# Row-wise argmax: the last tiles in column pieces with a VectorE lookup, and 128 chunks of 64 elements per row in place of 64 of 128

## The chip, the cores and the metric

The kernel runs on one core of a Trainium2 chip. The metric is the device time of one execution in microseconds (us); each kernel was executed several times, and this text quotes medians. The profile of one execution gives the span, from the first to the last instruction, which here is about 1.8 us shorter than the device time.

Names: VectorE is DVE in the profile, GpSimd is POOL, ScalarE is ACT, TensorE is PE, SyncE's queue is SPq. "xt" is a tile of input: 128 rows of 8192 float32, 4 MB. There are 64 such tiles, 0 to 63.

## The reference

```python
def setup_inputs():
    return {"x": np.random.randn(8192, 8192).astype(np.float32)}

def reference(x):
    return np.argmax(x, axis=1)
```

The output is int64, so the kernel writes each index as a pair of int32 words, the upper one zero.

## The kernel before

A row is cut into C chunks of L = 8192 / C elements. VectorE reduces each tile to C chunk maxima per row (`cm`), in one instruction for the whole tile, and that is nearly all its work. Per group of four tiles, a lookup follows: the row maximum `mx`, the first chunk that holds it (GpSimd compares and multiplies with a descending ramp, VectorE takes the maximum `k`), an indirect DMA that fetches that one chunk per row from HBM again (`ga`), and the same match inside the chunk. Each step is put some tiles later in program order, so that VectorE does not wait for GpSimd or for the gather.

```python
C = 64;  L = M // C                      # 64 chunks of 128
groups = [4] * 15 + [2, 1, 1]
# (constants, buffers, keep(), some arguments, store() and the group's last step are cut)

def stage2(t0, g, cm, now):
    reduce_max(out=mx, in_=cm)                       # VectorE
    w, k = first_match(cm, mx, descC, C, g, "c")     # GpSimd, two operations per tile
    def stage3():                                    # one tile later
        reduce_max(out=k, in_=w)                     # VectorE
        tensor_tensor(out=idx, in0=base[:, t0:t0 + g], in1=k, op=ALU.subtract)
        for i in range(g):
            nc.gpsimd.indirect_dma_start(out=ga[:, i, :], in_=x_flat, ... idx[:, i:i + 1] ...)
        w2, k2 = first_match(ga, mx, descL, L, g, "l")
        # (stage4, four tiles later: reduce w2 to k2, combine with k into res; cut)

for g in groups:
    for i in range(g):
        parts = 4 if t == NT - 1 else 1              # only tile 63 is loaded in pieces
        # (one DMA per part into xt, then one reduce_max per part into cm)
        run_due(t)
        t += 1
    stage2(t0, g, cm, t - 1)
# (the rest of the steps, then transpose, cast and store of the last four tiles)
```

Five buffers hold tiles, so loads run up to five tiles ahead.

## Time and profile before

| | before |
|---|---|
| time, median of the first three runs (with a fourth, used below, 667.21) | 667.33 us (667.04 to 667.47) |
| span of the profiled run | 665.3 us |
| last x packet ends (the trace's DMA packets) | 639.8 us |
| last reduce of x ends | 648.1 us |
| from there to the end of the span | 17.2 us |

The first lines are from the page of the kernel before: the span, the busy tenths of VectorE and of the DMA engines in 40 slices of the span, and the two DMA queues with packets, megabytes and share of the 16 engines' time. Queue q1 carries x, q0 the gathers (half of q0's 2048 packets are of 4 bytes; the other 1024 carry the rows).

```profile
span 665.3 us, 723 instructions
...
DVE  2899898998989899898998989899898998989891
...
DMA  9999999999999999999999999999999999999930
...
q1 hardware_dynamic: 9731, 268.51, 94.5%
q0 software_dynamic: 2048, 4.20, 1.7%
```

The DMA engines are at 9 tenths for 38 slices and then nearly idle for the last two. VectorE is nearly as full, 8 or 9 tenths from the second slice to the last but one.

The groups by shape (line, engine, operation, output and input, count; busy us and mean ns of one; idle time just before them and what ended it):

```profile
L135 DVE TENSOR_REDUCE cm<-xt 128x64 f32<-128x8192 f32 x63 | 547.0, 8683 | 65.9 <-DMA xt<-in_x_dram 65.9
...
L135 DVE TENSOR_REDUCE cm<-xt 128x16 f32<-128x2048 f32 x4 | 8.9, 2274 | 0.0
```

A whole tile takes VectorE 8.68 us. A quarter takes 2.27 us; four in a row took 8.85 (in the timeline below), 0.17 more than a whole tile, because the records of successive reduces overlap a little. Taken at 0.96 GHz, 8192 elements are 8.53 us and 2048 are 2.13, which leaves 0.15 and 0.14 us per instruction. The Trainium skill ("VectorE: DVE Perf Modes", Specifications and the section on the TRN2 errata) gives that clock and a measured fixed term of about 150 cycles, 0.156 us; this trace agrees with both, to within 0.02 us.

The timeline of the tail (start, duration, engine, line, operation, count; in brackets the idle time before and what ended it):

```profile
630.11 8.69 DVE L135 TENSOR_REDUCE cm<-xt 128x64 f32<-128x8192 f32 x1 [2.05 <-DMA xt<-in_x_dram]
...
639.23 8.85 DVE L135 TENSOR_REDUCE cm<-xt 128x16 f32<-128x2048 f32 x4
...
649.93 1.05 POOL L102 DMA_INDIRECT ga<-in_x_dram,idx  x1 [4.57 <-DVE mx L93]
...
655.27 1.04 POOL L102 DMA_INDIRECT ga<-in_x_dram,idx  x1 [0.73 <-DVE idx L99]
...
658.00 0.62 POOL L63 TENSOR_SCALAR w<-ga,mx 128x128 f32<-128x128 f32 x1 [1.69 <-DMA ga<-in_x_dram,idx]
...
659.19 0.29 DVE L108 TENSOR_REDUCE k<-w 128x1 f32<-128x128 f32 x1 [2.90 <-POOL w L65]
...
660.38 0.26 ACT L88 CAST o<-ps 4x128 int32<-4x128 f32 x1 [10.47 <-PE ps L85]
```

Tile 62 is reduced from 630.11 on, the four pieces of tile 63 only behind it, until 648.08. Then the two last groups of one tile take their gathers in turn (649.93 and 655.27), each with a GpSimd match, and after the last come match, reduce, transpose, cast (660.38) and store.

### The profile page before, as it was taken

The page shows a single profiled execution, that of the slowest core. Times are in us where ns is not written, and L with a number is a line of the kernel's source. Part 1 is how long each engine was busy: PE and PEld are TensorE (multiplying, and loading weights), DVE is VectorE, ACT ScalarE, POOL GpSimd, SP SyncE. Part 2 cuts the span into 40 slices and gives each one's busy share as a digit, 9 for nine tenths or more (in the row PEclk, how much of TensorE's full clock was granted, in tenths as well). Part 3 has the DMA queues.
Part 4 walks back from the last instruction along what each step waited for, and adds up shares of the span by engine and source line. Part 5 has one row for each costly group of instructions (what it writes and reads, how often), then busy time and mean ns, then how long its engine had stood idle before and what let it go on. Part 6 is the DMA issues. An engine that isn't in the chain of part 4 may idle for free.

```text
span 665.3 us, 723 instructions
## 1 busy us (share of the span) xinstructions
PE 0.8 (0%) x2; PEld 0.2 (0%) x2; DVE 584.1 (88%) x175; ACT 1.8 (0%) x3; POOL 179.7 (27%) x331
## 2 busy tenths in 40 slices
PE   0000000000000000000000000000000000000000
PEld 0000000000000000000000000000000000000000
DVE  2899898998989899898998989899898998989891
ACT  0000000000000000000000000000000000000000
POOL 1004214041231304214032231304214131331442
DMA  9999999999999999999999999999999999999930
GB/s 378 441 428 425 424 441 426 426 431 420 439 426 428 426 426 440 423 430 420 430 423 442 431 418 430 425 440 418 430 431 426 439 421 430 428 426 439 405 161 12
DMA packets 11786, 272.75 MB, mean 410 GB/s; under 512 B 2116, under 2 KB 2180, under 8 KB 3204
## 3 DMA queue, kind: packets, MB, share of 16 engines
q1 hardware_dynamic: 9731, 268.51, 94.5%
q0 software_dynamic: 2048, 4.20, 1.7%
q14 instruction: 7, 0.05, 0.0%
HBM read 272.63 MB, written 0.07 MB: 410 GB/s over the span
## 4 chain that ended last, share of the span: by engine, by line
DMA 76%; DVE 19%; issue 3%; POOL 0%; SPq 0%; POOLq 0%; PE 0%; ACT 0%; DVEq 0%; ACTq 0%
DMA xt<-in_x_dram 75%; DVE cm L135 18%; DMA ga<-in_x_dram,idx 1%; DVE k L108 0%; SPq L132 0%; POOL w L63 0%; DVE mx L93 0%; DVE k L97 0%; DVE res L110 0%; POOL w L65 0%; DVE res L112 0%; POOLq L171 0%; DVE idx L99 0%; PE ps L85 0%; ACT o L88 0%
## 5 line engine op out<-in xcount | busy, mean ns | idle before, releaser
L135 DVE TENSOR_REDUCE cm<-xt 128x64 f32<-128x8192 f32 (+1 forms) x67 | 555.9, 8301 | 65.9 <-DMA xt<-in_x_dram 65.9
L63 POOL TENSOR_SCALAR w<-cm,mx 128x64 f32<-128x64 f32 x64 | 28.2, 441 | 261.4 <-DVE mx L93 261.4
L102 POOL DMA_INDIRECT ga<-in_x_dram,idx x64 | 62.4, 974 | 115.0 <-DVE idx L99 91.2
L63 POOL TENSOR_SCALAR w<-ga,mx 128x128 f32<-128x128 f32 x64 | 38.8, 606 | 91.7 <-DMA ga<-in_x_dram,idx 91.7
L65 POOL TENSOR_TENSOR w<-w,descL 128x128 f32<-128x128 f32 x64 | 29.1, 454 | 5.3
L65 POOL TENSOR_TENSOR w<-w,descC 128x64 f32<-128x64 f32 x64 | 20.4, 319 | 5.3
L108 DVE TENSOR_REDUCE k<-w 128x4 f32<-128x512 f32 (+2 forms) x18 | 11.1, 617 | 2.9 <-POOL w L65 2.9
L97 DVE TENSOR_REDUCE k<-w 128x4 f32<-128x256 f32 (+2 forms) x18 | 6.8, 379 | 4.8 <-POOL w L65 4.8
L93 DVE TENSOR_REDUCE mx<-cm 128x4 f32<-128x256 f32 (+2 forms) x18 | 6.9, 382 | 0.1
L99 DVE TENSOR_TENSOR idx<-base,k 128x4 uint32<-128x4 f32 (+2 forms) x18 | 2.9, 162 | 0.9 <-DVE k L97 0.3
L112 DVE TENSOR_SCALAR res<-res 128x4 f32<-128x4 f32 (+2 forms) x18 | 3.0, 168 | 0.6
L110 DVE SCALAR_TENSOR_TENSOR res<-k 128x4 f32<-128x4 f32 (+2 forms) x18 | 2.9, 162 | 0.6
L88 ACT CAST o<-ps 60x128 int32<-60x128 f32 (+1 forms) x2 | 0.5, 263 | 658.1 <-PE ps L85 658.1
L85 PE MATMUL ps<-ident,res 128*60 128x128 f32 (+1 forms) x2 | 0.8, 382 | 659.5 <-DVE k L97 649.2
L88 ACT ACT_TABLE_LOAD x1 | 1.3, 1283 | 0.7 <-PEq L160 0.7
L87 POOL MEMSET o<- 60x256 int32 (+1 forms) x2 | 0.6, 301 | 0.0
L55 POOL TENSOR_SCALAR ident<-ident 128x128 f32<-128x128 f32 x1 | 0.5, 534 | 0.0
L85 PEld LDWEIGHTS ps<-ident,res 128*60 128x60 f32 (+1 forms) x2 | 0.2, 104 | 659.8 <-issue 649.2
L42 POOL IOTA descC<- 128x64 f32 x1 | 0.2, 175 | 0.4 <-POOLq L160 0.4
L45 POOL IOTA descL<- 128x128 f32 x1 | 0.2, 228 | 0.0
L53 POOL IOTA ident<- 128x128 f32 x1 | 0.2, 228 | 0.0
L49 POOL IOTA base<- 128x64 f32 x1 | 0.2, 174 | 0.0
(4 smaller groups left out, 0.4 us busy)
## 6 DMA issues: line engine op xcount, KB each, us to landing
xt<-in_x_dram SPq DMA_DIRECT2D x63, 4096.0 KB, 41.0
xt<-in_x_dram SPq DMA_DIRECT2D x4, 1024.0 KB, 37.5
ga<-in_x_dram,idx POOLq DMA_INDIRECT x64, 8.6
out_dram<-o SPq DMA_DIRECT2D x1, 60.0 KB, 1.6
out_dram<-o SPq DMA_DIRECT2D x1, 4.0 KB
```

What stands on the lines that cost most here:

```text
L63: keep(nc.gpsimd.tensor_scalar(out=w[:, i, :], in0=vals[:, i, :], scalar1=mx[:, i:i + 1], scalar2=None, op0=ALU.is_equal))
L65: keep(nc.gpsimd.tensor_tensor(out=w[:, i, :], in0=w[:, i, :], in1=desc, op=ALU.mult))
L85: nc.tensor.transpose(ps, res[:, t0:t0 + n], ident)
L88: nc.scalar.copy(out=o[:, :, 0:1], in_=ps.unsqueeze(2))
L93: keep(nc.vector.reduce_max(out=mx, in_=cm, axis=AX.X))
L97: keep(nc.vector.reduce_max(out=k, in_=w, axis=AX.X))
L99: keep(nc.vector.tensor_tensor(out=idx, in0=base[:, t0:t0 + g], in1=k, op=ALU.subtract))
L102: keep(nc.gpsimd.indirect_dma_start(out=ga[:, i, :], out_offset=None, in_=x_flat[:, :], in_offset=bass.IndirectOffsetOnAxis(ap=idx[:, i:i ...
L108: keep(nc.vector.reduce_max(out=k2, in_=w2, axis=AX.X))
L110: keep(nc.vector.scalar_tensor_tensor(out=res[:, t0:t0 + g], in0=k, scalar=float(L), in1=k2, op0=ALU.mult, op1=ALU.add))
L112: keep(nc.vector.tensor_scalar(out=res[:, t0:t0 + g], in0=res[:, t0:t0 + g], scalar1=-1.0, scalar2=float(C * L + L), op0=ALU.mult, op1=ALU ...
L135: keep(nc.vector.reduce_max(out=cm[:, i, q * cw:(q + 1) * cw], in_=xt[:, q * w:(q + 1) * w].rearrange("p (c l) -> p c l", c=cw), axis=AX.X))
```

## The change

Its intent: (A) 128 chunks of 64, so that the gathers fetch half the bytes; (B) the last four tiles loaded and reduced in column pieces of 2048 and less, so that VectorE can start on a tile before all of it has landed; (C) tiles 62 and 63 looked up by VectorE alone (`max` and `max_index`), without GpSimd's matches, and tile 63 stored directly without a transpose. The core of the diff:

```diff
-    C = 64
+    C = 128
@@ load and reduce, in pieces @@
+    def load_reduce(t, cm, widths):
+        for w in widths:
+            keep(nc.sync.dma_start(out=xt[:, at:at + w], in_=x[t * P:(t + 1) * P, at:at + w]))
+        for w in widths:
+            keep(nc.vector.reduce_max(out=cm[:, c0:c1], in_=xt[:, at:at + w]..., axis=AX.X))
+            step[0] = t * 4 + at // 2048      # deferred steps now count quarter tiles
+            run_due()
@@ lookup of one tile on VectorE @@
+    def direct_begin(t, cm):
+        keep(nc.vector.max(out=m8, in_=cm))
+        keep(nc.vector.max_index(out=c8, in_max=m8, in_values=cm))
+        keep(nc.vector.tensor_tensor(out=idx, in0=c8[:, 0:1], in1=base[:, t:t + 1], op=ALU.add))
+        keep(nc.gpsimd.indirect_dma_start(out=ga, ..., in_=x_flat[:, :], ... idx ...))
+    def direct_end(m8, c8, ga, dst):
+        keep(nc.vector.max_index(out=l8, in_max=m8, in_values=ga))
+        keep(nc.vector.scalar_tensor_tensor(out=dst, in0=c8[:, 0:1], scalar=float(L), in1=l8[:, 0:1], ...))
@@ order @@
-    groups = [4] * 15 + [2, 1, 1]
+    for g in [4] * 15 + [2]:
+            load_reduce(t, cm[:, i, :], [M] if t < 60 else [2048] * 4)
+        lookup(t0, g, cm, 4, 7) if g == 4 else lookup(t0, g, cm, 1, 100)
+    load_reduce(62, cm62, [2048] * 4);                     d62 = direct_begin(62, cm62)
+    load_reduce(63, cm63, [2048] * 3 + [1024, 512, 512]);  d63 = direct_begin(63, cm63)
+    step[0] = 1000;  run_due()
+    direct_end(*d62, res[:, 62:63]);  store(60, 3)
+    direct_end(*d63, o_last[:, 0:1]); nc.sync.dma_start(out=out_pairs[63 * P:, :], in_=o_last)
```

More of the change, by code (lines that the diff above doesn't have):

```diff
@@ L35, with out_view @@
     oth = out.tensor
-    oth2 = type(oth)(name=oth.name, shape=[NT, 2 * P], dtype=I32, base_partition=oth.base_partition)
-    out_i32 = oth2.ap()
+    def out_view(shape):
+        return type(oth)(name=oth.name, shape=shape, dtype=I32, base_partition=oth.base_partition).ap()
+    out_rows = out_view([NT, 2 * P])
+    out_pairs = out_view([N, 2])
     x_flat = x.tensor.reshape([N * C, L]).ap()
@@ L48 @@
     base = cpool.tile([P, NT], F32)
-    nc.gpsimd.iota(out=base, pattern=[[P * C, NT]], base=C, channel_multiplier=C,
+    nc.gpsimd.iota(out=base, pattern=[[P * C, NT]], base=0, channel_multiplier=C,
+                   allow_small_or_imprecise_dtypes=True)
+    baseC = cpool.tile([P, NT], F32)
+    nc.gpsimd.iota(out=baseC, pattern=[[P * C, NT]], base=C, channel_multiplier=C,
                    allow_small_or_imprecise_dtypes=True)
@@ L57, with defer, run_due, match @@
     res = cpool.tile([P, NT], F32)
-    def first_match(vals, mx, desc, n, g, name):
-        w = spool.tile([P, g, n], F32, tag=f"w_{name}")
+    o_last = cpool.tile([P, 2], I32)
+    nc.gpsimd.memset(o_last, 0)
+    pending = []
+    step = [0]
+    def defer(steps, fn):
+        pending.append((step[0] + steps, fn))
+        pending.sort(key=lambda e: e[0])
+    def run_due():
+        while pending and pending[0][0] <= step[0]:
+            pending.pop(0)[1]()
+    def load_reduce(t, cm, widths):
+        assert sum(widths) == M
+        xt = xpool.tile([P, M], F32, tag="xt")
+        at = 0
+        for w in widths:
+            keep(nc.sync.dma_start(out=xt[:, at:at + w], in_=x[t * P:(t + 1) * P, at:at + w]))
+            at += w
+        at = 0
+        for w in widths:
+            c0, c1 = at // L, (at + w) // L
+            keep(nc.vector.reduce_max(
+                out=cm[:, c0:c1], in_=xt[:, at:at + w].rearrange("p (c l) -> p c l", l=L), axis=AX.X))
+            at += w
+            step[0] = t * 4 + at // 2048
+            run_due()
+    def match(w, vals, mx, desc, g):
         for i in range(g):
             keep(nc.gpsimd.tensor_scalar(out=w[:, i, :], in0=vals[:, i, :], scalar1=mx[:, i:i + 1],
-                                    scalar2=None, op0=ALU.is_equal))
+                                         scalar2=None, op0=ALU.is_equal))
             keep(nc.gpsimd.tensor_tensor(out=w[:, i, :], in0=w[:, i, :], in1=desc, op=ALU.mult))
-        k = spool.tile([P, g], F32, tag=f"k_{name}")
-        return w, k
-    groups = [4] * 15 + [2, 1, 1]
-    assert sum(groups) == NT
-    pending = []
-    def run_due(now, all_=False):
-        while pending and (all_ or pending[0][0] <= now):
-            pending.pop(0)[1]()
-    def defer(due, fn):
-        pending.append((due, fn))
-        pending.sort(key=lambda e: e[0])
     def store(t0, n):
@@ L85, in store, with lookup, gather @@
         nc.tensor.transpose(ps, res[:, t0:t0 + n], ident)
-        o = spool.tile([n, P, 2], I32, tag="o")
+        o = cpool.tile([n, P, 2], I32, tag=f"o{t0}")
         nc.gpsimd.memset(o, 0)
-        nc.scalar.copy(out=o[:, :, 0:1], in_=ps.unsqueeze(2))
-        keep(nc.sync.dma_start(out=out_i32[t0:t0 + n, :], in_=o.rearrange("t p two -> t (p two)")))
-    def stage2(t0, g, cm, now):
+        keep(nc.scalar.copy(out=o[:, :, 0:1], in_=ps.unsqueeze(2)))
+        keep(nc.scalar.dma_start(out=out_rows[t0:t0 + n, :], in_=o.rearrange("t p two -> t (p two)")))
+    def lookup(t0, g, cm, gather_after, match_after):
         mx = spool.tile([P, g], F32, tag="mx")
         keep(nc.vector.reduce_max(out=mx, in_=cm, axis=AX.X))
-        w, k = first_match(cm, mx, descC, C, g, "c")
-        def stage3():
-            keep(nc.vector.reduce_max(out=k, in_=w, axis=AX.X))
+        wc = spool.tile([P, g, C], F32, tag="wc")
+        match(wc, cm, mx, descC, g)
+        k = spool.tile([P, g], F32, tag="k")
+        def gather():
+            keep(nc.vector.reduce_max(out=k, in_=wc, axis=AX.X))
             idx = spool.tile([P, g], U32, tag="idx")
-            keep(nc.vector.tensor_tensor(out=idx, in0=base[:, t0:t0 + g], in1=k, op=ALU.subtract))
+            keep(nc.vector.tensor_tensor(out=idx, in0=baseC[:, t0:t0 + g], in1=k, op=ALU.subtract))
             ga = spool.tile([P, g, L], F32, tag="ga")
@@ L104, in stage3 @@
                     in_offset=bass.IndirectOffsetOnAxis(ap=idx[:, i:i + 1], axis=0)))
-            w2, k2 = first_match(ga, mx, descL, L, g, "l")
-            def stage4():
-                keep(nc.vector.reduce_max(out=k2, in_=w2, axis=AX.X))
-                keep(nc.vector.scalar_tensor_tensor(out=res[:, t0:t0 + g], in0=k, scalar=float(L),
-                                               in1=k2, op0=ALU.mult, op1=ALU.add))
-                keep(nc.vector.tensor_scalar(out=res[:, t0:t0 + g], in0=res[:, t0:t0 + g],
-                                        scalar1=-1.0, scalar2=float(C * L + L),
-                                        op0=ALU.mult, op1=ALU.add))
+            wl = spool.tile([P, g, L], F32, tag="wl")
@@ new lines, in gather, with finish @@
+            match(wl, ga, mx, descL, g)
+            def finish():
+                k2 = spool.tile([P, g], F32, tag="k2")
+                keep(nc.vector.reduce_max(out=k2, in_=wl, axis=AX.X))
+                r = res[:, t0:t0 + g]
+                keep(nc.vector.scalar_tensor_tensor(out=r, in0=k, scalar=float(L), in1=k2,
+                                                    op0=ALU.mult, op1=ALU.add))
+                keep(nc.vector.tensor_scalar(out=r, in0=r, scalar1=-1.0, scalar2=float(C * L + L),
+                                             op0=ALU.mult, op1=ALU.add))
@@ L115, in stage4 @@
                 if t0 + g == 60:
                     store(0, 60)
-            defer(now + 4, stage4)
-        defer(now + 1, stage3)
+            defer(match_after, finish)
+        defer(gather_after, gather)
+    def direct_begin(t, cm):
+        m8 = spool.tile([P, 8], F32, tag="m8")
+        keep(nc.vector.max(out=m8, in_=cm))
+        c8 = spool.tile([P, 8], U32, tag="c8")
+        keep(nc.vector.max_index(out=c8, in_max=m8, in_values=cm))
+        idx = spool.tile([P, 1], U32, tag="idx1")
+        keep(nc.vector.tensor_tensor(out=idx, in0=c8[:, 0:1], in1=base[:, t:t + 1], op=ALU.add))
+        ga = spool.tile([P, L], F32, tag="ga1")
+        keep(nc.gpsimd.indirect_dma_start(
+            out=ga, out_offset=None, in_=x_flat[:, :],
+            in_offset=bass.IndirectOffsetOnAxis(ap=idx[:, :1], axis=0)))
+        return m8, c8, ga
@@ L122 @@
+    def direct_end(m8, c8, ga, dst):
+        l8 = spool.tile([P, 8], U32, tag="l8")
+        keep(nc.vector.max_index(out=l8, in_max=m8, in_values=ga))
+        keep(nc.vector.scalar_tensor_tensor(out=dst, in0=c8[:, 0:1], scalar=float(L), in1=l8[:, 0:1],
+                                            op0=ALU.mult, op1=ALU.add))
     t = 0
-    for g in groups:
+    for g in [4] * 15 + [2]:
         cm = spool.tile([P, g, C], F32, tag="cm")
@@ L126 @@
         for i in range(g):
-            xt = xpool.tile([P, M], F32, tag="xt")
-            parts = 4 if t == NT - 1 else 1
-            w = M // parts
-            cw = C // parts
-            for q in range(parts):
-                keep(nc.sync.dma_start(out=xt[:, q * w:(q + 1) * w],
-                                  in_=x[t * P:(t + 1) * P, q * w:(q + 1) * w]))
-            for q in range(parts):
-                keep(nc.vector.reduce_max(
-                    out=cm[:, i, q * cw:(q + 1) * cw],
-                    in_=xt[:, q * w:(q + 1) * w].rearrange("p (c l) -> p c l", c=cw), axis=AX.X))
-            run_due(t)
-            t += 1
-        now = t - 1
-        stage2(t0, g, cm, now)
-    run_due(0, all_=True)
-    while pending:
-        run_due(0, all_=True)
-    store(60, NT - 60)
+            load_reduce(t, cm[:, i, :], [M] if t < 60 else [2048] * 4)
+            t += 1
+        if g == 4:
+            lookup(t0, g, cm, 4, 7)
+        else:
+            lookup(t0, g, cm, 1, 100)
+    cm62 = spool.tile([P, C], F32, tag="cm1")
+    load_reduce(62, cm62, [2048] * 4)
+    d62 = direct_begin(62, cm62)
+    cm63 = spool.tile([P, C], F32, tag="cm1")
+    load_reduce(63, cm63, [2048] * 3 + [1024, 512, 512])
+    d63 = direct_begin(63, cm63)
+    step[0] = 1000
+    run_due()
+    direct_end(*d62, res[:, 62:63])
+    store(60, 3)
+    direct_end(*d63, o_last[:, 0:1])
+    nc.sync.dma_start(out=out_pairs[63 * P:, :], in_=o_last)
 _INS = ['x']
```

## The prediction

> **What bounds it now.** Two stages. Until about 640 us the DMA engines are the limit: the table of 40 slices shows DMA at 9 tenths through slice 38, and the windows from 12 to 594 us show a DMA share of 1.00 to 1.01 at 426 to 431 GB/s, with VectorE busy 91%. In the groups by shape VectorE needs 8.68 us for a 4 MB row tile; a tile lands every 9.7 us; the idle time before it (65.9 us) all ends on xt. Then comes a serial tail of 26 us: in the trace's DMA packets the last x packet ends at 639.8 us, the span at 665.3. In the timeline that tail is VectorE reducing the last tile (639.2 to 648.1, as its four pieces queue behind tile 62, reduced whole until 638.8), two gather rounds in turn (649.9 and 655.3), POOL matches, a transpose, a cast, a store, and 4.6 us from the cast to the end.
>
> **Part A, chunks of 64.** VectorE and POOL hardly change: 128x256 to 128x4 took 0.41 us, 128x512 to 128x4 0.68, so a group of four tiles gains one such 0.27 us; VectorE has 1 us of slack per tile. The row reduce should stay at 8.7 us. What matters is the gather: half the bytes on a saturated DMA. Today's 1024 gather packets (4 KB each) take 0.17 us each, 10.9 us per engine in all. The Trainium skill ("DMA: Bandwidth & Descriptors", "Why small descriptors are slow") gives a 256-byte descriptor 11 cycles, 8 of data and 3 of overhead. By that rule 512 bytes take 19, and gathers fall to 11/19, some 6.3 us: an estimated gain of 4.6 us, all on the critical path. The same page says that transfers under 512 bytes are read-modify-write; if so, the gain may be zero. I count 3.5.
>
> **Part B, pieces.** The loads of tiles 60 to 63 become 8 KB and smaller packets. Today's 8 KB packets took 0.317 us against 1.225 for 32 KB, so some 1.3 us of DMA is lost. Net: the last byte at about 637.5 us.
>
> **Part C, tail.** A quarter-tile reduce is 2.27 us against 2.5 us of its load, so VectorE keeps up, with a backlog: lookups are inserted, and the wait for POOL's match of tiles 60 and 61 may stall it 1 to 2.5 us (POOL does four gathers and eight matches first; today that took 15 us). Estimated after the last byte: last reduce with backlog 2.0; Max, MaxIndex, add and issue gap 1.1 (from 0.28 us for a 128-element reduce); gather 2.7 (today 655.27 to 658.00); MaxIndex and multiply-add 0.5; store 1.5; fixed end 3.7 (today from the store's landing). Sum 11.5 us in place of 25.5.
>
> **Time.** 637.5 + 11.5 = 649 us of span, plus 2 between span and time: 651 us, ratio 1.025. Range 647.5 to 655. Faster by over 2% needs under 654.2: 0.82; same 0.17; slower 0.01.
>
> **What would show it.** Gather packets of about 0.10 us in place of 0.17, steady tiles 9.64 us apart instead of 9.71. Last x packet near 637.5. Last reduce ending within 2 us of it. One gather after it, no POOL match, and the span ending 9 to 10 us after that reduce. Before tile 62's second piece, an idle VectorE ended by POOL.
>
> **What would make it wrong.** Small descriptors that save nothing or delay x; a larger backlog because POOL is late (the gather of tile 62 queues behind it too); a chunked reduce that slows with more rows; MaxIndex costing far more than a reduce of its length; a slow store of 8-byte rows.

## More of the kernel before

All executions quoted are of the fast state, with a granted clock of 1.00.

Nothing but VectorE's pace decides when a landed tile is reduced.

A tile lands every 9.94 us (first reduce of tile 0 at 12.95 us, tile 59 landed at 599.61).

## The result, and the profile after

The changed kernel took 655.68 us (655.41 to 655.96, four runs) against 667.21 us. The ratio is 0.9827, with a 95% interval of 0.981 to 0.9844. A ratio is the mean time of one kernel's fast runs over that of the other's of the same rounds, so it is not quite the ratio of the medians. At 1.7% it is faster beyond noise, but inside the band of 2%. The prediction had said 651.0 us, 647.5 to 655.0, and "faster by over 2%" with a chance of 0.82: it was wrong, by 4.7 us.

The page after, the same lines:

```profile
span 653.8 us, 739 instructions
...
DVE  2899898998989989998998989989998998989986
...
DMA  9999999999999999999999999999999999999980
...
q1 hardware_dynamic: 11376, 268.44, 96.3%
q0 software_dynamic: 2048, 2.10, 0.9%
```

The DMA engines now finish in slice 39 of a shorter span. Queue q0 carries half the bytes in about half the share. And VectorE, which used to rest in the last slice, is now full almost to the end, which is the first sign of what happened. The groups by shape after:

```profile
L92 DVE TENSOR_REDUCE cm<-xt 128x128 f32<-128x8192 f32 x60 | 521.2, 8686 | 51.5 <-DMA xt<-in_x_dram 51.5
...
L92 DVE TENSOR_REDUCE cm<-xt 128x32 f32<-128x2048 f32 x15 | 33.4, 2276 | 0.0
```

The whole-tile reduce with 128 outputs takes what the one with 64 took (8.686 us against 8.683): twice as many chunks cost the row reduce nothing. The second line holds the answer: fifteen quarter reduces, and an idle time before them of 0.0. VectorE never once waited for a piece. Yet pieces help only an engine that is waiting for data.

The timeline from the landing of tile 59 on:

```profile
595.34 8.69 DVE L92 TENSOR_REDUCE cm<-xt 128x128 f32<-128x8192 f32 x1 [0.45 <-DMA xt<-in_x_dram]
...
604.66 8.86 DVE L92 TENSOR_REDUCE cm<-xt 128x32 f32<-128x2048 f32 x4
...
614.23 8.86 DVE L92 TENSOR_REDUCE cm<-xt 128x32 f32<-128x2048 f32 x4
...
623.46 2.28 DVE L92 TENSOR_REDUCE cm<-xt 128x32 f32<-128x2048 f32 x1
...
627.39 0.42 DVE L122 TENSOR_REDUCE k<-wc 128x2 f32<-128x256 f32 x1 [1.66 <-POOL wc L103]
...
627.92 4.47 DVE L92 TENSOR_REDUCE cm<-xt 128x32 f32<-128x2048 f32 x2
...
633.02 2.28 DVE L92 TENSOR_REDUCE cm<-xt 128x32 f32<-128x2048 f32 x1
...
636.24 8.97 DVE L92 TENSOR_REDUCE cm<-xt 128x32 f32<-128x2048 f32 x6
...
645.25 0.29 DVE L152 MAX8 m<-cm 128x8 f32<-128x128 f32 x1
...
646.40 0.94 POOL L158 DMA_INDIRECT ga<-in_x_dram,idx  x1 [8.76 <-DVE k L135]
...
648.82 0.09 DVE L165 MATCH_VALUE_LOAD l<-m,ga 128x8 f32 x1 [1.64 <-DMA ga<-in_x_dram,idx]
...
649.38 0.35 SPq L192 DMA_DIRECT2D out_dram<-o_last  x1
```

Beside it, when the first piece of each tile had landed (the last of the 16 completion counts of its DMA in the trace) and when VectorE started on it:

| first piece of tile | landed, us | reduce starts, us | lag, us |
|---|---|---|---|
| 60 | 597.80 | 604.66 | 6.9 |
| 61 | 607.74 | 614.23 | 6.5 |
| 62 | 617.68 | 623.46 | 5.8 |
| 63 | 628.91 | 636.24 | 7.3 |

The last x packet ended at 636.3 us, and the last reduce at 645.2 (636.24 + 8.97), 8.9 us later. VectorE was busy from 595.34 to there with one pause of 1.66 us, ahead of the reduce at 627.39, which waited for GpSimd. After it the new tail is short: 8.6 us in place of 17.2.

### The profile page after: what moved, and what is told of

Its sections match the earlier page's. It is cut to its first block, busy times and chain, and to the rows that moved or that the text cites. A ratio compares the mean times of both kernels' runs of the same rounds, so it can differ in the third digit from the quotient of the medians.

```text
span 653.8 us, 739 instructions
## 1 busy us (share of the span) xinstructions
PE 0.8 (0%) x2; PEld 0.2 (0%) x2; DVE 592.0 (91%) x188; ACT 1.8 (0%) x3; POOL 176.0 (27%) x325
## 3 DMA queue, kind: packets, MB, share of 16 engines
q0 software_dynamic: 2048, 2.10, 0.9%
## 4 chain that ended last, share of the span: by engine, by line
DMA 77%; DVE 19%; issue 2%; POOL 1%; SPq 0%; POOLq 0%; DVEq 0%
DMA xt<-in_x_dram 76%; DVE cm L92 18%; DMA ga<-in_x_dram,idx 1%; POOL ga L127 0%; SPq L87 0%; POOL wc L101 0%; POOL ga L158 0%; DVE k L122 0%; POOL wc L103 0%; DVE mx L116 0%; POOL wl L101 0%; DVE k L135 0%; DVE c L154 0%; DVE idx L124 0%; POOL wl L103 0%
## 5 line engine op out<-in xcount | busy, mean ns | idle before, releaser
L92 DVE TENSOR_REDUCE cm<-xt 128x128 f32<-128x8192 f32 (+2 forms) x78 | 556.9, 7152 | 51.5 <-DMA xt<-in_x_dram 51.5
L101 POOL TENSOR_SCALAR wc<-cm,mx 128x128 f32<-128x128 f32 x62 | 37.2, 601 | 256.3 <-DVE mx L116 256.3
L101 POOL TENSOR_SCALAR wl<-ga,mx 128x64 f32<-128x64 f32 x62 | 27.6, 445 | 98.2 <-DMA ga<-in_x_dram,idx 98.2
L103 POOL TENSOR_TENSOR wc<-wc,descC 128x128 f32<-128x128 f32 x62 | 28.1, 453 | 5.2
L103 POOL TENSOR_TENSOR wl<-wl,descL 128x64 f32<-128x64 f32 x62 | 19.7, 319 | 5.2
L122 DVE TENSOR_REDUCE k<-wc 128x4 f32<-128x512 f32 (+1 forms) x16 | 10.6, 660 | 1.7 <-POOL wc L103 1.7
L116 DVE TENSOR_REDUCE mx<-cm 128x4 f32<-128x512 f32 (+1 forms) x16 | 10.7, 669 | 0.6
L135 DVE TENSOR_REDUCE k<-wl 128x4 f32<-128x256 f32 (+1 forms) x16 | 6.4, 400 | 0.0
L140 DVE TENSOR_SCALAR res<-res 128x4 f32<-128x4 f32 (+1 forms) x16 | 2.7, 170 | 0.6
L138 DVE SCALAR_TENSOR_TENSOR res<-k,k 128x4 f32<-128x4 f32 (+1 forms) x16 | 2.7, 167 | 0.6
```

What stands on the lines that cost most here:

```text
L92: keep(nc.vector.reduce_max(out=cm[:, c0:c1], in_=xt[:, at:at + w].rearrange("p (c l) -> p c l", l=L), axis=AX.X))
L101: keep(nc.gpsimd.tensor_scalar(out=w[:, i, :], in0=vals[:, i, :], scalar1=mx[:, i:i + 1], scalar2=None, op0=ALU.is_equal))
L103: keep(nc.gpsimd.tensor_tensor(out=w[:, i, :], in0=w[:, i, :], in1=desc, op=ALU.mult))
L116: keep(nc.vector.reduce_max(out=mx, in_=cm, axis=AX.X))
L122: keep(nc.vector.reduce_max(out=k, in_=wc, axis=AX.X))
L135: keep(nc.vector.reduce_max(out=k2, in_=wl, axis=AX.X))
```

## The experiments

Theory: the inherited lag. A tile that is reduced whole can be started only when all of it has landed, and then takes 8.7 us, in which most of the next tile lands. So VectorE enters the first tile in pieces 6.9 us behind its first piece (the expectations below put this lag at 7.3). In pieces it needs about 2.2 us (four took 8.86) for what takes about 2.49 us to load, and the lookups eat that surplus. It stays behind to the end.

Rivals: the backlog is made inside the last four tiles, by the inserted lookups and the wait for GpSimd; or the small packets bring x late and VectorE merely follows; or the smaller chunks cost VectorE more. Rounds marked by the same value of "before" ran on the same chip; the changed kernel ran in rounds of its own, so a difference from it crosses rounds, in which "before" stayed within 0.2 us. The 95% interval of each ratio is about 0.0015 to either side, some 1 us. "Behind" is the end of the last reduce less the end of the last x packet; "tail" is from there to the end of the span.

| run | time, us | before, us | ratio | last x packet, us | behind, us | tail, us |
|---|---|---|---|---|---|---|
| before | 667.21 | | | 639.8 | 8.3 | 17.2 |
| after | 655.68 | 667.21 | 0.9827 | 636.3 | 8.9 | 8.6 |
| e1_chunks_only | 662.28 | 667.26 | 0.9924 | 635.4 | 8.7 | 16.5 |
| e2_tail_only | 659.34 | 667.26 | 0.9882 | 641.5 | 7.4 | 8.6 |
| e3_last4_half_reduce | 648.04 | 667.26 | 0.9710 | 636.9 | 0.9 | 8.6 |
| e4_tile59_half_reduce | 651.01 | 667.26 | 0.9759 | 636.4 | 4.2 | 8.6 |
| e5_pieces_from_56 | 653.26 | 667.07 | 0.9793 | 637.4 | 5.7 | 8.3 |
| e6_no_stall | 653.95 | 667.07 | 0.9802 | 636.2 | 7.3 | 8.9 |
| e9_halves_44_59 | 652.31 | 667.07 | 0.9777 | 638.2 | 4.0 | 8.5 |
| e10_combined | 650.88 | 667.07 | 0.9755 | 638.3 | 2.5 | 8.5 |
| e11_halves_from_52 | 650.52 | 667.25 | 0.9747 | 637.8 | 2.6 | 8.3 |

The first row already says it: the kernel before had the same 8.3 us. The prediction's own reading, that the pieces of tile 63 "queue behind tile 62", had been a view of it.

### e1_chunks_only: part A alone

```diff
 # the kernel before
-    C = 64
+    C = 128
```

> The kernel before with 128 chunks of 64 and nothing else. Both theories of the tail (VectorE a whole tile late, or late data) expect the loads to end some 4.7 us sooner, because the gathers move half the bytes (gather packets 0.087 us in place of 0.170), and the old tail behind them to keep its 25.5 us, plus 0.1 for the longer 128-element operations: 662.5 us. If the smaller gathers had helped only in company with the new tail: 667.

Measured: 662.28 us, 5.0 us faster than before. The gather packets of the trace took a mean of 0.091 us in place of 0.170, the last x packet came 4.4 us sooner, and the tail was 16.5 us. The saturated DMA gives back the time of the bytes that the gathers no longer move, and that time comes through.

### e2_tail_only: parts B and C alone

```diff
 # the changed kernel
-    C = 128
+    C = 64
```

> The changed kernel with 64 chunks of 128: the new tail and pieces alone. If the chunk change is worth its 4.7 us of DMA time and the backlog of VectorE in the last four tiles does not depend on it: 660.3 us, with the last reduce again 8 to 9 us behind the last byte. If the chunked reduce with twice as many outputs were what holds VectorE back, the quarter reduces would be shorter here (under 2.2 us) and the time nearer to 656.

Measured: 659.34 us, 7.9 us faster than before, with the last reduce 7.4 us behind the last packet (a little less than the 8 to 9 expected). The quarter reduces stayed at 2.28 us, so the number of chunks is not what holds VectorE back. The two parts, 5.0 and 7.9 us, add up to 12.9, while together they gave 11.5. That fits a last stretch paced by VectorE: once tile 59 has landed, a faster load is worth nothing more there, and the 128-chunk lookups on VectorE are longer (0.69 against 0.42 us for `mx` of four tiles, for one).

### e3_last4_half_reduce: half the reduce work in the last four tiles

```diff
 # the changed kernel; the result is wrong on purpose
-    in_=xt[:, at:at + w].rearrange("p (c l) -> p c l", l=L), axis=AX.X))
+    in_=xt[:, at:at + w].rearrange("p (c l) -> p c l", l=L)[:, :, 0:(L // 2 if t >= 60 else L)],
+    axis=AX.X))
```

> The changed kernel, reducing only the first half of every chunk in tiles 60 to 63 (a wrong result on purpose). VectorE-bound theory: a piece takes 1.2 us in place of 2.28, VectorE catches up with the loads within about seven pieces, the last reduce ends 0.5 to 1.5 us after the last byte (636.3 us) in place of 8.9, and the time falls by about 8 us to 647.7. Late-data theory (small packets delay x, VectorE merely follows): the reduces are shorter but the last one ends where it did, 655.5.

Measured: 648.04 us. VectorE in the timeline:

```profile
604.88 4.59 DVE L92 TENSOR_REDUCE cm<-xt 128x32 f32<-128x1024 f32 x4
...
612.94 1.22 DVE L92 TENSOR_REDUCE cm<-xt 128x32 f32<-128x1024 f32 x1 [0.21 <-DMA xt<-in_x_dram]
616.21 1.22 DVE L92 TENSOR_REDUCE cm<-xt 128x32 f32<-128x1024 f32 x1 [2.05 <-DMA xt<-in_x_dram]
...
637.35 0.42 DVE L92 TENSOR_REDUCE cm<-xt 128x8 f32<-128x256 f32 x1 [0.22 <-DMA xt<-in_x_dram]
```

From the seventh piece on (612.94) it waits for loads again and again, as the brackets show, and the last reduce ends 0.9 us behind the last packet. The loads were not late: they came at 636.9 us, no sooner than in the changed kernel. That rules out the theory of late data, and it shows the floor for this tail: about 648 us, if VectorE were not behind (a little low, as its last piece took 0.42 us here in place of 0.67).

### e4_tile59_half_reduce: 4.3 us less work, 40 us before the end

```diff
 # the changed kernel; the result is wrong on purpose; as e3, but
+    ... [:, :, 0:(L // 2 if t == 59 else L)]
```

> The changed kernel with the one reduce of tile 59 halved (wrong result on purpose), 40 us before the last byte. Theory of the inherited lag (VectorE enters tile 60 a whole-tile reduce behind, 7.3 us, and has no surplus to make it up): all 4.3 us come through to the end, 651.4 us, last reduce 4.6 us behind the last byte. Rival (the backlog is made inside the last four tiles by the inserted lookups and the wait for POOL): VectorE has nothing to do with the time won and waits for the first piece, 654.8 to 655.7.

Measured: 651.01 us, 4.7 us less than the changed kernel (in other rounds; the ratios to before are 0.9759 and 0.9827).

```profile
595.38 4.42 DVE L92 TENSOR_REDUCE cm<-xt 128x128 f32<-128x4096 f32 x1 [0.46 <-DMA xt<-in_x_dram]
...
600.43 8.85 DVE L92 TENSOR_REDUCE cm<-xt 128x32 f32<-128x2048 f32 x4
...
619.22 2.28 DVE L92 TENSOR_REDUCE cm<-xt 128x32 f32<-128x2048 f32 x1
622.92 0.42 DVE L124 TENSOR_REDUCE k<-wc 128x2 f32<-128x256 f32 x1 [1.42 <-POOL wc L105]
...
631.68 8.98 DVE L92 TENSOR_REDUCE cm<-xt 128x32 f32<-128x2048 f32 x6
```

The one reduce takes 4.42 us in place of 8.69. The first piece of tile 60 starts at 600.43 in place of 604.66, and the last six at 631.68 in place of 636.24. Nothing between has soaked up the 4.3 us, so VectorE had been behind from the start of tile 60. The rival that the backlog arises in the last four tiles expected at most 0.9 us here; it falls as the main cause. It keeps a part, though: the first piece of tile 62 had landed at 618.83 and was started at 619.22, so only 0.4 us of lag was left there, and yet the last reduce is 4.2 us behind. Most of that arises in tiles 62 and 63 themselves, where VectorE again waits for GpSimd (1.42 us) and does lookups.

### e5_pieces_from_56: pieces four tiles earlier

```diff
-            load_reduce(t, cm[:, i, :], [M] if t < 60 else [2048] * 4)
+            load_reduce(t, cm[:, i, :], [M] if t < 56 else [2048] * 4)
```

> The changed kernel with pieces from tile 56 in place of 60. Inherited-lag theory: tile 56 inherits the same lag, and VectorE, which needs 9.1 us for a tile in pieces and 0.5 for lookups against 9.9 of load, is then busy without a pause from tile 55 on: it gains only the pauses between tiles 56 and 59 less the extra 0.17 us per tile, some 1.8 us, 653.9 us; the loads end 1.3 us later, which costs nothing because they do not bind. If earlier pieces cure the backlog outright (what one hopes of pieces): the last reduce within 2 us of the last byte, 650 us. If the backlog is made in the last four tiles and the small packets are what counts: 657 us.

Measured: 653.26 us, 2.4 us less than the changed kernel. Tile 56 inherits the same lag, and VectorE then runs on without a pause until it meets the same GpSimd wait (1.73 us).

```profile
625.41 0.42 DVE L122 TENSOR_REDUCE k<-wc 128x2 f32<-128x256 f32 x1 [1.73 <-POOL wc L103]
```

Pieces let it use the pauses of four more tiles and no more: the last reduce is still 5.7 us behind, although the loads end 1.1 us later.

### e6_no_stall: without the wait for GpSimd

```diff
-            lookup(t0, g, cm, 1, 100)
+            lookup(t0, g, cm, 3, 100)
```

> The changed kernel with the index step of tiles 60 and 61 placed after the third piece of tile 62 in place of the first, so that VectorE does not wait for POOL. VectorE-bound theory: the pause of 1.66 us vanishes and all of it comes off the time, 654.0 us. If something else ends last: 655.5.

Measured: 653.95 us, 1.7 us less than the changed kernel, which is the whole pause. (The intervals of the two ratios just touch, 0.9786 to 0.9819 and 0.981 to 0.9844; that the gain is this pause rests on the timeline too.)

```profile
623.46 6.66 DVE L92 TENSOR_REDUCE cm<-xt 128x32 f32<-128x2048 f32 x3
...
630.76 0.41 DVE L122 TENSOR_REDUCE k<-wc 128x2 f32<-128x256 f32 x1
...
634.47 8.97 DVE L92 TENSOR_REDUCE cm<-xt 128x32 f32<-128x2048 f32 x6
```

Three quarter reduces of tile 62 now run without a pause between them (623.46), the index step `k` comes after them without an idle time, and the last six pieces start 1.8 us sooner. So the prediction's wait for GpSimd was real and rightly sized ("1 to 2.5 us"), and it was the small part.

### e9_halves_44_59: catch up slowly, beforehand

```diff
-            load_reduce(t, cm[:, i, :], [M] if t < 60 else [2048] * 4)
+            load_reduce(t, cm[:, i, :], [M] if t < 44 else [4096] * 2 if t < 60 else [2048] * 4)
```

> The changed kernel with tiles 44 to 59 loaded and reduced as two halves (16 KB packets). Inherited-lag theory: VectorE needs 8.82 us plus 0.5 of lookups for such a tile against 9.8 of load, so over 16 tiles the lag at the start of tile 60 falls from 7.3 us to about 3; the packets cost an estimated 0.1 us per tile, 1.7 in all; net 653.1 us. Rival (backlog made in the last four tiles): only the packets count, 657.4 us.

Measured: 652.31 us, 3.4 us less than the changed kernel.

```profile
447.04 8.73 DVE L92 TENSOR_REDUCE cm<-xt 128x64 f32<-128x4096 f32 x2
...
502.63 4.42 DVE L92 TENSOR_REDUCE cm<-xt 128x64 f32<-128x4096 f32 x1 [0.57 <-DMA xt<-in_x_dram]
...
601.82 8.86 DVE L92 TENSOR_REDUCE cm<-xt 128x32 f32<-128x2048 f32 x4
...
620.61 2.28 DVE L92 TENSOR_REDUCE cm<-xt 128x32 f32<-128x2048 f32 x1
...
633.25 8.97 DVE L92 TENSOR_REDUCE cm<-xt 128x32 f32<-128x2048 f32 x6
```

The first half of tile 44 had landed at 442.59 and was reduced from 447.04 on, a lag of 4.5 us. From there VectorE runs without waiting for a load until the first half of tile 50 (502.63; the expectation of e11 below says tile 49): its small surplus needs 55 us, the six tiles 44 to 49, to work that lag off. The change to quarters brings a smaller lag of its own, as the last half is still being reduced when the first quarter lands: that of tile 60 had landed at 599.21 and was started at 601.82, 2.6 us later. This is still earlier than the 604.66 of the changed kernel, although the loads are later. At tile 62 the lag is gone (landed 620.55, started 620.61), and the last reduce is 4.0 us behind in place of 8.9. The price shows in the last packet, 1.9 us later: a packet of 16 KB took 0.619 us, so two of them 1.237 against 1.226 for one of 32 KB.

### e10_combined and e11_halves_from_52: a version that beats both

```diff
 # e10; e11 has 52 in place of 44
+            load_reduce(t, cm[:, i, :], [M] if t < 44 else [4096] * 2 if t < 58 else [2048] * 4)
-        lookup(t0, g, cm, 4, 7)              # and: lookup(t0, g, cm, 1, 100)
+        lookup(t0, g, cm, 4, 7 if t0 < 56 else 100)   # and: lookup(t0, g, cm, 3, 100)
-    store(0, 60) after tile 59's group; store(60, 3) at the end
+    store(0, 56) after tile 55's group; store(56, 7) at the end
```

> A version meant to beat both: halves in tiles 44 to 57, quarters from 58, the index step of tiles 60 and 61 after the third piece of tile 62, the last step of tiles 56 to 59 moved behind the last gather, where VectorE waits anyway. Inherited-lag theory: the last reduce ends 2 to 3 us behind the last byte, which comes at about 638.4; 8.6 us of tail; 651.4 us. Rival: 656 to 658, as the loads take longer.

> The combined version with halves in tiles 52 to 57 only. In the run with halves from tile 44 VectorE first waited for a load again in tile 49, six tiles on, so six tiles of halves should just be enough; eight tiles fewer in 16 KB packets save an estimated 0.1 us each of load time. Inherited-lag theory: last byte 0.8 us sooner, last reduce still 2 to 3.5 us behind it, 650.2 us (649.8 to 651.0). If six tiles are too few, VectorE never pauses in tiles 58 to 63 and the time is 651 to 652.

Measured: 650.88 us and 650.52 us, both correct, and both over 2% faster than the kernel before. VectorE in e10:

```profile
607.99 2.29 DVE L92 TENSOR_REDUCE cm<-xt 128x32 f32<-128x2048 f32 x1 [0.19 <-DMA xt<-in_x_dram]
...
618.42 2.29 DVE L92 TENSOR_REDUCE cm<-xt 128x32 f32<-128x2048 f32 x1 [0.64 <-DMA xt<-in_x_dram]
...
625.99 2.29 DVE L92 TENSOR_REDUCE cm<-xt 128x32 f32<-128x2048 f32 x1 [0.20 <-DMA xt<-in_x_dram]
...
631.82 9.00 DVE L92 TENSOR_REDUCE cm<-xt 128x32 f32<-128x2048 f32 x6
```

and in e11:

```profile
612.53 2.29 DVE L92 TENSOR_REDUCE cm<-xt 128x32 f32<-128x2048 f32 x1 [0.66 <-DMA xt<-in_x_dram]
```

In e10 it now waits for pieces, for 0.19 us, then 0.64 and 0.20: it has caught up with the loads, and the last reduce ends 2.5 us behind the last packet. What each of the changes in e10 gave by itself was not measured. The times of e10 and e11 are not told apart: their intervals overlap (0.9738 to 0.9771 and 0.9734 to 0.976). In e11 the last packet came 0.45 us sooner, where 0.8 was expected. Its six tiles of halves did not quite do: VectorE entered the quarters of tile 58 2.3 us behind (landed 578.64, started 580.95), and the first wait that its timeline shows is in tile 61 (612.53).

## Why the prediction was wrong

The span, term by term:

| term | predicted, us | measured, us |
|---|---|---|
| last x packet | 637.5 | 636.3 |
| last reduce ends, after that | 2.0 | 8.9 |
| Max, MaxIndex, add and issue gap | 1.1 | 1.2 |
| gather | 2.7 | 2.4 |
| MaxIndex and multiply-add | 0.5 | 0.5 |
| store and end | 1.5 + 3.7 | 4.5 |
| span | 649 | 653.8 |

(Measured from the timeline after: 645.21 to 646.40, to 648.82, to 649.31, to 653.8.)

- **The step that failed** is, as the prediction put it, "A quarter-tile reduce is 2.27 us against 2.5 us of its load, so VectorE keeps up, with a backlog", sized at "last reduce with backlog 2.0". Both rates are right. What was left out is where VectorE stood when the pieces began: 6.9 us behind the first of them, because tile 59 is reduced whole after it has landed. With a surplus near 0.3 us per piece and some 3 us of lookups and 1.7 of waiting on the way, this could not be made up in 18 pieces. The term was 8.9 us, 6.9 more than the estimate (that this is also the lag at tile 60 is chance). Experiment e3 shows that the term was VectorE's work, and e4 that the larger part was inherited: it took 4.3 us off, and 0.4 were left at tile 62. By an estimate from e4, then, some 4.7 of the 8.9 us were inherited and 4.2 arise in tiles 62 and 63; e9, in which the lag was gone at tile 62 and the last reduce still 4.0 behind, agrees. So the 2.0 was too small for this second part as well. Of it, the wait for GpSimd is 1.7 us (e6), and 0.9 is left even with short reduces (e3); the rest was not taken apart.
- **Part A was right in kind and a little too low.** It counted 3.5 us and estimated 4.6; part A alone gave 5.0 (e1). The steady tiles came closer together, 9.94 us to 9.87 (tile 0 to tile 59; the absolute figures in the prediction, 9.71 and 9.64, had left out the tiles that also carry gathers). The Trainium skill ("DMA: Bandwidth & Descriptors", Why small descriptors are slow) led to 11/19 of the packet time, 0.098 us; measured was 0.087 of 0.170, 0.51. The page puts the 3 cycles of overhead on a packet, and the prediction had charged them to each row, while a gather packet here carried eight rows (1024 packets for 8192 rows). Counted per packet, the page's figures give 67 of 131 cycles (8 x 8 + 3 for the small rows, 8 x 16 + 3 for the large), 0.51: an estimate made afterwards, which fits. The doubt taken from the same page, that transfers under 512 bytes are read-modify-write and may gain nothing, was not borne out here.
- **Part B's cost was near**: 8 KB packets took 0.316 us each in the changed kernel, and its last packet came 0.9 us later than with part A alone (636.3 against 635.4), where 1.3 was predicted.
- **Part C's chain was right**: one gather, no GpSimd match after it, and 8.6 us from the last reduce to the end, where the prediction said "9 to 10". The idle VectorE ended by GpSimd was where it was foretold, ahead of the second piece of tile 62, and within its range (1.66 us, against 1 to 2.5).
- **The range** was too narrow on the side of the one term that had been argued from rates and not traced back in the timeline. That the time was off by only 4.7 us is in part luck: the last packet came 1.2 us sooner and the steps after the last reduce took 0.9 less than predicted (8.6 against 9.5), which hid 2.1 of the 6.9 us.

## What to carry to other kernels

When you cut work into pieces so that it overlaps its loads, work out how far behind the consumer is when the first piece lands, and not only whether its rate is higher; a consumer that takes whole tiles is a whole tile's work behind. If both engines are near full, the lag goes away only at the rate of the difference, here 4.5 us in six tiles, so the cutting must begin that much earlier, in the coarsest pieces that do it; a later change to finer pieces starts with a smaller lag again (2.6 us in e9, 2.3 in e11). An idle time of 0.0 before the new pieces tells at once that they had nothing to wait for.

## What the Trainium skill lacked or had wrong

- "DMA: Bandwidth & Descriptors", Specifications: it says that transfers under 512 bytes are read-modify-write and off line rate. For gathered reads from HBM into SBUF no such step is seen: 1024 packets carry 8192 gathered rows, eight each; eight rows of 512 bytes took 0.170 us, eight of 256 bytes 0.087 (24.1 and 23.6 bytes per ns), about what one contiguous row of 2 KB took (0.091).
- The same page, Measured, tables whole transfers. What was needed here is the time of one packet by row length: 32 KB 1.226 us, 16 KB 0.619, 8 KB 0.316, 4 KB 0.165, 2 KB 0.091.
- The same page, Where 436 GB/s comes from: it says that about 358 GB/s of HBM per core binds for HBM to SBUF. With one core at work these runs held 426 to 431 GB/s for 580 us. The page's own Measured section has 425 for a single core and keeps the 358 for two cores streaming at once; its 425 fits.
- No page has durations for Max8 and for MaxIndex. Here Max8 took 0.29 us on 128 elements and 0.23 on 64; MaxIndex is two instructions, 0.09 us to load the values and 0.28 to search 128 elements, or 0.22 for 64.
